# One pool per kind of tile, the rare path at the kernel's end, and the first attention in other PSUM banks

## The chip, the cores and the metric

The kernel runs on one core of a Trainium2 chip. Times are device microseconds (us) of one execution of the whole program. The engines are TensorE (PE in the profile, with PEld its weight loads), VectorE (DVE), ScalarE (ACT), GpSimd (POOL) and SyncE (SP), which issues nearly all transfers. Each engine works through its own list of instructions in order and waits on semaphores for the others. Engine names with a q behind them (PEq, SPq) stand for the engine's sequencer: branches, register loads and DMA issues.

## The reference

One layer of a hybrid decoder: 4096 tokens of width 1024, three mixers in parallel on one normalised input, then one output projection.

```python
def _hybrid_layer(x, c_act, ...):
    shift, scale, gate = jnp.split(c_act @ ada_w + ada_b, 3, axis=-1)
    h = _rmsnorm(x, g_pre) * (1.0 + scale[:, None]) + shift[:, None]
    aq, ak, av, ag, rkv, rg, gq, gkk, gv, gg = jnp.split(h @ w_in, ...)
    attn = _sliding_window_attention(aq, ak, av, sinks) * jax.nn.silu(ag)     # window 128, 8 heads of 64, 2 kv heads
    rwkv = _rwkv7_mixer(h, ...) * jax.nn.silu(rg)                             # a recurrence over the tokens, 4 heads
    gla = _gla_mixer(h, gq, gkk, gv, gk1, gk2, gk_b, gla_norm_w) * jax.nn.silu(gg)
    y = jnp.concatenate([attn, rwkv, gla], axis=-1) @ w_out
    return x + gate[:, None] * _rmsnorm(y, g_post)
```

RWKV-7 and GLA carry a state along the 4096 tokens; the attention looks at most 128 tokens back, with a sink per head in its softmax.

## The kernel before

The 4096 rows are worked through in 16 steps (NS) of 256 rows (NT). **Phase one** does for each step the normalisation (hT, the transposed input, is also stored in HBM), the projections of the two recurrent mixers, GLA, and RWKV-7 in chunks of 64 tokens. Of RWKV-7 the prediction names these pieces. PE forms products AT; these go through HBM (`adr`) into the layout AS; DVE solves a triangular system in a loop of small steps (`tsc`, `TT`); the result goes through HBM again (`tdr`, `td`); DVE transposes it (`D`), PE multiplies it out (`Xp`, `Xq`, `X`), and stage q2 runs four chained chunks (`rp`, `up`, `sp`) that carry the state. At its end DVE normalises `ysb`, PE transposes it (`yt`), ACT scales it, DVE adds the bonus `bon`, and the result of the step is stored (`mscr`). The last `yt`, of step 15, is thus the last that the recurrence asks of PE. Phase one also writes the weights of phase two to HBM in two f16 halves, high and low (`wscr`, `woscr`).

**Phase two** loads these weights (`stage_w`, L1594: q0 to q6, of which q5 and q6 lie in a pool of their own, `wg`) and does for each step: `qkv` (L1636: keys kp, queries qp in two halves with q0 and q1, values vp with q2; the values go through HBM, `vscr`, into four blocks v), `gates` (L1688: products gp with q3 to q6, tanh on ACT and one multiply on DVE into `ag`), `stage_s` (L1705: for each half a of the step the scores sc, a reduction on DVE that adds the bias `ab` and finds the maximum m, exponentials on ACT, division and transposes on DVE, and the product with the values, ovp), `stage_m` (L1790: the mixers' outputs times the gates, a scale found with a small product mp, and a split into f16 blocks `mtp`) and `outp` (L1877: seven products op per step in place of eight, combined on DVE in yv, normalised and stored).

The work is written as generators, one per stage, which `streams` and `emit` (L551) run interleaved by a model of the banks and the clock. Every instruction is noted by `Order`, whose `pin` (L205) fixes each engine's order by a list schedule with the kernel's own costs; it is called once for phase one and once for the loop of phase two. Step 0's attention, the projections of steps 0 and 1 and the gates of step 0 (`stage_first`) lie between the two; their places come from the scheduler of the framework, which puts them among the instructions of phase one as far as their tiles' ground, their banks and the barriers allow. Since the calls go through one helper, nearly all instructions carry its line, L334.

Tiles of SBUF come from pools. A pool of phase two that lies over ground of phase one can be filled when the tiles beneath are done with. Phase one has four pools by hand-made groups (`work1a` to `work1d`) and `c1p`; phase two has seven, each with several kinds of tiles. PSUM banks go by tags: `pj` (two), `at`, `sq`, `tr`, `m`, `y`, `mq`. Stage q2 uses `sq` and `y`.

A flag `fi` says if GLA's gates stay within a limit. If they don't (in none of the runs here), a **fallback** computes GLA again token by token, stores it to `mscr`, and loads again the three weight tiles that it used as work space. Its place is between the first attention and the loop of phase two: `values_load(fi)` at L2013, the branch at L2029, its loop at L2037. All engines pass the branch.

Of the kernel before, what the change touches and what calls it, by code (L numbers as in the profile page):

```python
# [11 lines left out]
F16 = mybir.dt.float16  # L12
# [284 lines left out]
class Model:  # L297


    def __init__(self, tc):  # L300
        self.tc, self.lift, self.stage, self.order = tc, 0, None, Order(tc)
        self.wrote, self.read, self.banks = {}, {}, {}
        self.now = self.pipe = 0.0
        self.shared = True
        self.gate = None
# [93 lines left out]
def hybrid_kernel(ctx, tc, x, vecs, rows, ada1, adaw, w1, wl, w2, wo, w2aug, a2, gk2, cst, ctr, ctg, abias, out):  # L399
# [84 lines left out]
    def pst(tag, name, bufs=1):  # L484
        t = ps.tile([P, 512], F32, tag=tag, name=name, bufs=bufs)
        model.take(tag, bufs, t.tensor.name)
        return t
# [67 lines left out]
    def emit():  # L555

        while live:
# [13 lines left out]
            model.lift, model.stage = LIFT.get(best[2], 0), best[2]  # L571
# [73 lines left out]
    with ExitStack() as p1:  # L645

        wk1 = [pool_of(p1, f"work1{n}", 1) for n in "abcd"]
        pp = pool_of(p1, "c1p", 1)
        order = (("hf", "gl", "b1", "zs", "gw", "cgc", "bl", "gk1s", "zl0", "zl1", "zl2", "ch", "cl", "cs"),
                 ("zb0", "zb1", "zb2", "ta", "ep", "em", "b2", "KB"),  # L650
                 ("qg", "kg", "egp", "egm", "vg", "c2", "kt", "cd", "em0"))

        def wt(shape, name, bufs=1, dt=F32, tag=None):
            tag = tag or name
            n = next((n for n, tags in enumerate(order) if tag in tags), 3)
            return wk1[n].tile(shape, dt, tag=tag, name=name, bufs=bufs)
# [68 lines left out]
        gvh = wk1[0].tile([P, KD, 272], F16, name="gvh")  # L725
        gvl = wk1[0].tile([P, KD, 272], F16, name="gvl")
# [850 lines left out]
    w2k, pp, wg, w2m, w2p, w2o, wb = [pool2(n) for n in ("work2k", "c2p", "wg", "work2m", "work2p", "work2o", "wb")]  # L1577
    pools = {"q": w2k, "kT": w2k, "vt": w2k, "v4": w2k, "mxa": w2m, "mxb": w2m, "pr": w2p, "yv": w2o, "sm1": w2o}
# [7 lines left out]
    ab = pp.tile([P, 8, 256], BF16, name="ab")  # L1586
# [7 lines left out]
    def stage_w(_):  # L1594
# [4 lines left out]
        for n in order:  # L1599
            slot = wslot if n < 5 else lambda name: wg.tile([P, KD, 256], F16, name=name)  # L1600
            got[n] = load_2(n, slot(f"q{n}h"), slot(f"q{n}l"))
            if n == 1:
                load_h(1)
# [32 lines left out]
    def qkv(i):  # L1636
# [10 lines left out]
        lohi = (slice(0, 64), slice(64, 128))  # L1647
        if i > 0:
            G.tensor_copy(kT[:, :, :, 0:P], F[i - 1]["kT"][:, :, :, NT : NT + P])
        yield ["pj"]  # L1650
        kp = pjt("kp")
# [10 lines left out]
        for n in range(2):  # L1662
            yield ["pj"]
            qp = pjt("qp")
# [9 lines left out]
        yield ["mq"]  # L1674
        vp = mq("vp")
# [5 lines left out]

        SP.dma_start(vscr[i].rearrange("(a p) c -> p a c", p=P), vt_)
# [3 lines left out]
        done.add(("qkv", i))  # L1686

    def gates(i):  # L1688
        yield [("og", i - 1)]
        f = F[i]  # L1690
        ag = t_A([P, 8, NT], "ag") if i == 0 else F[0]["ag"]
        f["ag"] = ag
        for n in range(4):
            yield ["pj"]
            gp_ = pjt("gp")
            for b in range(2):
                yield from proj(gp_[:, b * NT : (b + 1) * NT], Wq[3 + n], b * P, P, f["hT"])
# [5 lines left out]
        done.add(("gates", i))  # L1703

    def stage_s(i):  # L1705
# [4 lines left out]
        yield [q, kT, "at", "sq"]  # L1710
# [3 lines left out]
        for a in range(2):  # L1714
            first = i == 0 and a == 0
            k0 = P if first else 0
            pr = [wt([P, 4, 256], "pr", 3) for _ in range(2)]
            m = st.tile([P, 8], F32, tag="m", name="m")
            for jp in range(2):
                for kv in range(2):  # L1720
                    sc = pst(("at", "sq")[kv], "sc").rearrange("p (j n) -> p j n", j=2)
                    for jj in range(2):
                        for z in range(2):
                            PE.matmul(sc[:, jj, k0:], q[:, kv, 2 * jp + jj, a * P : (a + 1) * P],
                                      kT[:, kv, z, a * P + k0 : a * P + 256], start=(z == 0), stop=(z == 1))
                    for jj in range(2):
                        h = kv * 4 + 2 * jp + jj
                        V.tensor_tensor_reduce(pr[kv][:, 2 * jp + jj, k0:], sc[:, jj, k0:], ab[:, h, k0:], scale=1.0,
                                               scalar=sinks[:, h : h + 1], op0=ALU.add, op1=ALU.max,
                                               accum_out=m[:, h : h + 1])  # L1730
                if jp == 0:
                    yield ["at", "sq"]
            nm = st.tile([P, 8], F32, tag="nm", name="nm")
            V.tensor_mul(nm, m, fneg)
            es = st.tile([P, 8], F32, tag="es", name="es")
            V.tensor_sub(es, sinks, m)
            V.tensor_mul(es, es, lsc)
            sm = st.tile([P, 8], F32, tag="sm", name="sm")
            for h in range(8):
                S.activation(pr[h // 4][:, h % 4, k0:], pr[h // 4][:, h % 4, k0:], AF.Exp, bias=nm[:, h : h + 1],  # L1740
                             scale=lsc[:, h : h + 1], accum_out=sm[:, h : h + 1])
                if h % 2:
                    yield [sm]
            S.activation(es, es, AF.Exp)
            V.tensor_add(sm, sm, es)
            rd = st.tile([P, 8], F32, tag="rd", name="rd")
            V.reciprocal(rd, sm)
            for h in range(8):
                V.tensor_scalar(pr[h // 4][:, h % 4, k0:], pr[h // 4][:, h % 4, k0:], rd[:, h : h + 1], None, op0=ALU.mult)
                if h % 4 == 3:  # L1750
                    yield [pr[h // 4]]

            pT = []
            for kv in range(2):
                pT.append(wt([P, 4, 256], "pr", 3))
                if first:
                    for j in range(4):
                        V.transpose(pT[kv][:, j, k0:], pr[kv][:, j, k0:])
                else:
                    V.transpose(pT[kv].rearrange("p j n -> p (j n)"), pr[kv].rearrange("p j n -> p (j n)"))  # L1760
            tags = ("tr", "m", "y", "mq")
            yield [*pT, *v4, *tags]
            ov = [pst(tag, "ovp")[:, 0:P].rearrange("p (j n) -> p j n", j=4) for tag in tags]

            lo = 4 if first else 0
            joint()
            for d in range(5):
                for n in range(4):
                    if n + d < lo:
                        continue  # L1770
                    vt_, z = vblk[a + (n + d) // 4], (n + d) % 4
                    for kv in range(2):
                        PE.matmul(ov[n][kv * 64 : kv * 64 + 64], vt_[32 * n : 32 * n + 32, z, kv * 64 : kv * 64 + 64],
                                  pT[kv][32 * n : 32 * n + 32, :, 32 * (n + d) : 32 * (n + d) + 32],
                                  start=(n + d == max(lo, n)), stop=(d == 4))
            joint(False)
            for n in range(4):
                S.copy(mx[:, 0:4, a * P + 32 * n : a * P + 32 * n + 32], ov[n])
            yield ["at", "sq"]

    def block(i, n):
# [6 lines left out]
        V.scalar_tensor_tensor(t[:, 1], f["src"][n], f["msc"], t[:, 0], op0=ALU.mult, op1=ALU.subtract)  # L1788

    def stage_m(i):  # L1790
# [25 lines left out]
        mp = mq("mp")  # L1816
        PE.matmul(mp[:, 0:2], ones, mss, start=True, stop=True)
        mtot = st.tile([P, 1], F32, tag="mtot", name="mtot")
        V.tensor_reduce(mtot, mp[:, 0:2], axis=AX.X, op=ALU.add)
        msc = f["msc"] = st.tile([P, 1], F32, tag="msc", name="msc")  # L1820
        miv = st.tile([P, 1], F32, tag="miv", name="miv")
        pow2(msc, miv, mtot)
        oi = f["oi"] = st.tile([P, 1], F32, tag="oi", name="oi")
        V.tensor_mul(oi, miv, w_inv[7])
# [26 lines left out]
    def last_square(f, h, part, sums):  # L1851
# [3 lines left out]
        S.activation(f["junk"][:, 0:512], f["yv"][h][:, cols], AF.Square, scale=f["oi32"], accum_out=sums[:, part : part + 1])  # L1855
        V.tensor_tensor(z[:, cols], f["yv"][h][:, cols], gn[:, cols], op=ALU.mult)
# [20 lines left out]
    def outp(i):  # L1877
# [5 lines left out]
        yv = [wt([P, D], "yv", 2) if i < NS - 1 else  # L1883
# [35 lines left out]
        if end:  # L1919
            f["yv"], (f["junk"], *f["end"]) = yv, [wt([P, 4, 256], "pr", 3).rearrange("p j n -> p (j n)") for _ in range(3)]  # L1920
# [30 lines left out]
        else:  # L1951
            norm(i, 1, yv[1], x2[:, 0:D], f["blk"][5])
# [6 lines left out]
        else:  # L1959
            norm(i, 0, yv[0], x2[:, 0:D], f["blk"][6])  # L1960
        done.add(("o", i))

    def norm(i, a, yv, xt, junk):
        oi = F[i]["oi"]
# [39 lines left out]
    for n, stays in PRODUCTS:  # L2004
        if stays:
            Wr[n] = wb.tile([P, KD // 2, 4, 2, P], F16, name=f"o{n}")
# [165 lines left out]
```

## Time and profile before

| | before |
|---|---|
| median of 3 runs | 2091.4 us (2088.39 to 2092.16) |
| the profiled execution's own time | 2093.64 us |
| its span | 2091.8 us |
| mean granted clock of PE | 0.978 |
| PE busy | 1961.3 us, 94% of the span |
| DVE busy | 1612.5 us, 77% |
| ACT busy | 1154.3 us, 55% |

The profile is of one execution. A row of the timeline has start, duration, engine, line, operation, output and inputs, shape and, in brackets, how long the engine had been idle and who released it. A row of the waits has the waiting instruction, the releaser, the sum in us, the count and the longest. A matmul's own duration is longer than the distance to the next, since they are pipelined. Phase one lasts to about 1094 us, the loop of phase two from about 1133 us.

### The profile page before, as it was taken

To read this page: it belongs to the slowest core of one execution; us is meant where nothing else is said; L and a number is where in the kernel's file an instruction comes from. 1 tells how busy PE (TensorE), PEld (TensorE's weight loads), DVE (VectorE), ACT (ScalarE), POOL (GpSimd) and SP (SyncE) were. 2 spreads that over 40 slices of the span, in tenths; PEclk is the share of its full clock that TensorE was granted. 3 is DMA by queue.
4 is the path that set the end of the run, shared out by engine and by line. 5 is a ranking of instruction groups with operands and counts; after the bars stand their busy time and mean duration, and the time that the engine had idled before them with its cause. 6 is when DMAs were issued, how large, how long until landed. Compare 5 with 4: busy or idle time off the path is not lost. (4 is left out here: it accounts for less than half of the span.)

```text
span 2091.8 us, 61571 instructions
## 1 busy us (share of the span) xinstructions
PE 1961.3 (94%) x24931; PEld 1521.0 (73%) x24931; DVE 1612.5 (77%) x5211; ACT 1154.3 (55%) x2765; POOL 216.3 (10%) x405
## 2 busy tenths in 40 slices
PE   5899999999999999999876999999999999999997
PEld 2677778787787778777655767777877777877783
DVE  5677888878877688987745888777778777778777
ACT  4867676677776866765424444534444444344543
POOL 0511121421111111111100000000000000000000
PEclk9899999999999999999978999999999999999999
DMA  9332233323323312444116343433343433343314
GB/s 334 127 94 84 73 102 93 97 94 110 93 84 101 113 56 75 118 151 143 41 54 193 129 157 105 135 104 123 112 144 114 135 105 114 113 143 119 130 44 172
DMA packets 183894, 241.95 MB, mean 116 GB/s; under 512 B 52195, under 2 KB 141748, under 8 KB 179382
## 3 DMA queue, kind: packets, MB, share of 16 engines
q1 hardware_dynamic: 183462, 237.45, 35.2%
q8 instruction: 197, 3.23, 0.6%
q14 instruction: 91, 0.75, 0.1%
q10 hardware_dynamic: 144, 0.52, 0.1%
HBM read 177.08 MB, written 60.82 MB: 114 GB/s over the span
## 5 line engine op out<-in xcount | busy, mean ns | idle before, releaser
L334 PEld LDWEIGHTS <-mtp 128*128 128x128 f16 x1344 | 130.3, 98 | 141.3 <-issue 3.4
L334 PE MATMUL op<-o,mtp 128*128 128x512 f16 x768 | 172.1, 379 | 0.1
L334 ACT ACTIVATE pr<-pr,nm,lsc 128x256 f32<-128x256 f32 (+1 forms) x256 | 149.2, 585 | 36.0 <-DVE nm L334 35.9
L334 PE MATMUL op<-ov,mtp 128*128 128x512 f16 x576 | 143.4, 379 | 0.5 <-DVE q L334 0.5
L334 PEld LDWEIGHTS <-hT 128*128 128x128 f16 x1536 | 119.0, 100 | 25.9 <-issue 4.0
L334 DVE CUSTOM_DVE_ANT_0 pr<-sc,ab,sinks 128x256 f32<-128x256 f32 (+1 forms) x256 | 108.0, 475 | 14.1 <-PE sc L334 11.5
L334 DVE TENSOR_TENSOR yv<-op,yv 128x512 f32<-128x512 f32 x105 | 70.4, 681 | 48.6 <-PE op L334 34.3
L334 PE MATMUL pv<-gvh,hT 128*128 128x272 f16 x512 | 98.8, 283 | 6.6 <-DVE kg L334 3.1
L334 ACT ACTIVATE ag<-gp,gh 128x512 f32<-128x512 f32 x64 | 43.7, 683 | 102.8 <-PE gp L334 102.8
L334 POOL COPY kT<-kT 128x512 f16<-128x512 f16 x15 | 9.7, 646 | 872.7 <-DVE kT L334 820.5
L334 ACT ACTIVATE mtp<-yv,oi 128x1024 f16<-128x1024 f32 x30 | 34.3, 1143 | 112.6 <-DVE yv L334 112.6
L334 PE MATMUL lp<-hT,Lh 128*128 128x256 f16 x512 | 93.5, 276 | 0.1
L334 PE MATMUL gp<-hT,q3h 128*128 128x256 f16 x512 | 87.5, 275 | 4.4 <-PEq L2029 3.5
L334 PE MATMUL gp<-hT,q5h 128*128 128x256 f16 x512 | 91.1, 279 | 0.1
L334 PE MATMUL zz<-hT,rh 128*128 128x256 f16 x512 | 90.8, 277 | 0.0
L334 PE MATMUL zz<-hT,vh 128*128 128x256 f16 x512 | 88.8, 273 | 1.9 <-DVE zb L334 1.9
L334 PE MATMUL zz<-hT,kh 128*128 128x256 f16 x512 | 89.8, 273 | 0.0
L334 PE MATMUL gqk<-hT,gqkh 128*128 128x256 f16 x512 | 89.6, 276 | 0.0
L334 DVE SCALAR_TENSOR_TENSOR ag<-ag,gp 128x512 f32<-128x512 f32 x64 | 43.7, 683 | 58.5 <-ACT ag L334 58.2
L334 PE MATMUL qp<-hT,q0h 128*128 128x256 f16 x512 | 85.3, 273 | 2.3 <-DVE yv L334 1.5
L334 PE MATMUL qp<-hT,q1h 128*128 128x256 f16 x512 | 86.2, 273 | 0.0
L334 PE MATMUL gp<-hT,q6h 128*128 128x256 f16 x512 | 85.3, 273 | 0.0
(460 smaller groups left out, 6048.5 us busy)
## 6 DMA issues: line engine op xcount, KB each, us to landing
ov<-woscr SPq DMA_DIRECT2D x96, 512.0 KB, 4.0
xt<-in_x SPq DMA_DIRECT2D x16, 1024.0 KB, 5.1
hscr<-hT SPq DMA_DIRECT2D x16, 1024.0 KB, 5.0
hT<-hscr SPq DMA_DIRECT2D x16, 1024.0 KB, 4.8
x<-in_x SPq DMA_DIRECT2D x30, 512.0 KB, 4.5
out<-yv SPq DMA_DIRECT2D x30, 512.0 KB, 2.9
cs<-in_w SPq DMA_DIRECT2D x112, 128.0 KB, 2.4
v<-vscr SPq DMA_DIRECT2D x128, 64.0 KB, 2.6
```

The source lines that it names most:

```text
L334: r = f(*args, **kw)
```

## The change

**Pools.** Both phases now have one pool for each kind of tile. The pools of phase one stand in a list, and those of phase two in another, so that phase two's tiles lie over particular tiles of phase one: `q` over gvh and gvl, the weights q5 (`w5`) over b1, gl, bl, cs, ch, gw, the weights q6 (`w6`) over gw, zs and gaw, and so on. `yv` moves to ground that the input's tiles had (`t_A`), `mtp` to a pool.

**Banks.** Step 0's attention has its scores in `at` and `tr` in place of `at` and `sq`, and its ovp in `at`, `tr`, `m`, `mq` in place of `tr`, `m`, `y`, `mq`. The values vp of steps 0 and 1 use `pj`.

**Gates.** There are two buffers for `ag`; `gates(i)` asks that the gating of step i−2 be done, where it asked for i−1.

**Fallback.** It stands behind the loop of phase two. As the output is by then computed, it does all of phase two again as well, after GLA. For that `attend`, `heads_of`, `gates_of`, `spread_values` and `mix_scale` are made functions of their own, and `norm` gets its destination as an argument; the work they do in the main path is that of before.

```diff
     with ExitStack() as p1:
-        wk1 = [pool_of(p1, f"work1{n}", 1) for n in "abcd"]
-        pp = pool_of(p1, "c1p", 1)
-        order = (("hf", "gl", "b1", "zs", "gw", "cgc", "bl", "gk1s", "zl0", "zl1", "zl2", "ch", "cl", "cs"),
...
+        soon = ("w2s", "w0s", "a2s", "CT", "CTG", "scolb", "uw", "w0p0", "w0p1", "one16", "mu_s", "mu_c", "a0h")
+        late = ("td", "tf0", "tf1", "Sst0", "Sst1", "lnx")
+        tags = ("gvh", "gvl", "hf", "b1", "gl", "bl", "cs", "ch", "gw", "zs", "gaw", "gacc", "zl0", "zl1", "zl2", "early",
+                "zb1", "ta", "em", "ep", "zb0", "b2", "zb2", "kg", "kt", "egm", "egp", "qg", "vg", "c2", "middle",
+                "AS", "osb", "c3", "KB", "ATm", "c1", "RA", "UV", "BK", "cd", "em0", "bon", "ysb", "rs", "Ss", "lasts")
+        wk1 = {n: pool_of(p1, f"work1{n}", 1) for n in tags}
...
-    w2k, pp, wg, w2m, w2p, w2o, wb = [pool2(n) for n in ("work2k", "c2p", "wg", "work2m", "work2p", "work2o", "wb")]
-    pools = {"q": w2k, "kT": w2k, "vt": w2k, "v4": w2k, "mxa": w2m, "mxb": w2m, "pr": w2p, "yv": w2o, "sm1": w2o}
+    pools = {n: pool2("work2" + n) for n in (
+        "q", "kT", "vt", "w5", "w6", "ab", "v4", "pr", "mxa", "ag", "mtp", "mxb", "sm1", "o1", "o6", "o4", "o5", "ov")}
...
-            slot = wslot if n < 5 else lambda name: wg.tile([P, KD, 256], F16, name=name)
+            slot = wslot if n < 5 else lambda name: pools[f"w{name[1]}"].tile([P, KD, 256], F16, name=name)
...
     def gates(i):
-        yield [("og", i - 1)]
+        yield [("og", i - 2)]
         f = F[i]
-        ag = t_A([P, 8, NT], "ag") if i == 0 else F[0]["ag"]
-        f["ag"] = ag
+        f["ag"] = ag = t_A([P, 8, NT], "ag") if i == 0 else pools["ag"].tile([P, 8, NT], F32, name="ag2") if i == 1 else F[i - 2]["ag"]
+        yield from gates_of(f["hT"], ag, pjt)
...
     def stage_s(i):
         yield [("qkv", i), ("s", i - 1), ("o", i - 2)]
-        yield [q, kT, "at", "sq"]
+        sct, ovt = (("at", "tr"), ("at", "tr", "m", "mq")) if i < 1 else (("at", "sq"), ("tr", "m", "y", "mq"))
+        yield [q, kT, *sct]
...
         for a in range(2):
+            yield from attend(q, kT, vblk, mx, a, i == 0 and a == 0, sct=sct, ovt=ovt)
...
+    model.order.forget()
+    x2 = t_x("x2")
+    xo, gn = x2[:, 0, :], x2[:, 1, :]
+    mtp = pools["mtp"].tile([P, 4, 2, 4, P], F16, name="mtp")
...
+    streams((0, "v", stage_v, None), *((1, "s", stage_s, i) for i in range(1, NS)), *((2, "m", stage_m, i) for i in range(NS)),
+            *((3, "p2", stage_p2, i) for i in range(NS)))
+    emit()
+    model.order.pin()
 
     flag = nc.values_load(fi[0:1, 0:1], min_val=0, max_val=1)
...
     with tc.If(flag == 0):
...
-        for t, n in tiles_o[:3]:
-            load_o(t, n)
...
+        with tc.For_i(0, NS, 1) as iv:
+            SP.dma_start(fh.rearrange("p a k t -> p (a k t)"), hscr[bass.ds(iv, 1)].rearrange("o p n -> p (o n)"))
+            run(heads_of(fh, fq, fkT, fvt, pjt, mq))
+            spread_values(fvt, fv[1:], 0)
+            run(gates_of(fh, F[0]["ag"], pjt))
...
```

What this does to the order of the instructions shows at three places. The first is **SP**, around the triangular solve of step 14 and ahead of that of step 15. Before, with the loads of q5 and q6 only behind the `td` of step 15:

```order
L334 DMA adr<-AT 16x8x16 x5
L334 DMA AS<-adr 64x256 x2
L334 DMA q3h<-wscr 128x2048
L334 DMA q3l<-wscr 128x2048
L334 DMA q4h<-wscr 128x2048
...
L334 DMA td<-tdr 16x8x16 x8
L334 DMA adr<-AT 16x8x16 x8
L334 DMA AS<-adr 64x256 x2
...
L334 DMA td<-tdr 16x8x16 x2
L334 DMA q5h<-wscr 128x2048
```

After the change:

```order
L334 DMA adr<-AT 16x8x16 x5
L334 DMA q5h<-wscr 128x2048
L334 DMA q5l<-wscr 128x2048
L334 DMA AS<-adr 64x256 x2
L334 DMA q3h<-wscr 128x2048
...
L334 DMA vscr<-vt 128x2x128
L334 DMA v_18959<-vscr 32x4x128
L334 DMA adr<-AT 16x8x16 x8
L334 DMA v_18959<-vscr 32x4x128 x3
L334 DMA AS<-adr 64x256 x2
L334 DMA v_18960<-vscr 32x4x128 x4
```

The load of q5 now stands between step 14's adr and its AS, and the values of step 0 are stored and loaded around step 15's. The second place is **PE**, at the end of step 0's attention, where the branch stood:

```order
L334 MATMUL sc<-kT,q 128x256
L334 MATMUL ovp<-pr,v_18758 64x128 x14
L334 MATMUL ovp<-pr,v_18759 64x128 x2
...
L334 MATMUL ovp<-pr,v_18759 64x128 x14
L2013 TENSOR_LOAD fi
L2029 COMPARE_AND_BRANCH
```

In the changed kernel the second half's ovp follows the values of step 1, and other work follows it:

```order
L334 MATMUL qp<-hT,q1l 128x256
L334 LDWEIGHTS hT
L334 MATMUL vp<-q2h,hT 128x128
...
L334 MATMUL vp<-q2h,hT 128x128
L334 MATMUL ovp<-pr,v_18959 64x128 x14
L334 MATMUL ovp<-pr,v_18960 64x128 x2
```

The third is **DVE**, in the last normalisation of ysb, that of step 15. Before:

```order
L334 SCALAR_TENSOR_TENSOR ag<-ag,gp 128x512
L334 TENSOR_TENSOR ysb<-ysb,yr 128x512
L334 TENSOR_TENSOR ysb<-ysb,bon 128x512
L334 SCALAR_TENSOR_TENSOR kT<-kp,kq_s,kT 64x256 x4
L334 ISA pr,m<-sc,ab,sinks 128x128
```

The same place of DVE in the changed kernel:

```order
L334 SCALAR_TENSOR_TENSOR kT<-kp,kq_s,kT 64x256
L334 SCALAR_TENSOR_TENSOR yr<-nwt,yr 128x8
L334 SCALAR_TENSOR_TENSOR kT<-kp,kq_s,kT 64x256
L334 TENSOR_TENSOR nwt<-yr 128x8
L334 SCALAR_TENSOR_TENSOR nwt<-nwt,ve 128x8
L334 SCALAR_TENSOR_TENSOR yr<-nwt,yr 128x8
L334 TENSOR_TENSOR ysb<-ysb,yr 128x512
L334 SCALAR_TENSOR_TENSOR q<-qp,q 64x512
L334 TENSOR_TENSOR ysb<-ysb,bon 128x512
L334 SCALAR_TENSOR_TENSOR q<-qp,q 64x512
L334 ISA pr,m<-sc,ab,sinks 128x256
```

Splits of keys, which came behind the recurrence, now stand between the small instructions of its normalisation (`nwt`, `yr`), and the reductions (ISA) after it are those of the second half; the first half's stand earlier, in the triangular loop of step 15. From the first gate product with q3 behind the second mp on, the order of PE is the same in both until the last step; there it differs a little.

274 lines of the change are left out of this document (161 added, 113 removed).

## The prediction

> **What bounds the kernel now.** I read the page's busy shares first, then its 40 slices, then the windows table to find where TensorE (PE) loses time.
>
> ```profile
> span 2091.8 us, 61571 instructions
> PE 1961.3 (94%) x24931; PEld 1521.0 (73%) x24931; DVE 1612.5 (77%) x5211; ACT 1154.3 (55%) x2765; POOL 216.3 (10%) x405
> PE   5899999999999999999876999999999999999997
> PEclk9899999999999999999978999999999999999999
> ...
> 1000.00:1100.00 100.00, 80.85 (x1276) 61.30 (x1275) 53.78 (x195) 30.31 (x67) 7.58 (x14) 0.85 0.14 40
> 1100.00:1200.00 100.00, 81.81 (x881) 63.52 (x879) 72.53 (x225) 44.16 (x124) 1.71 (x2) 0.90 0.49 160
> 1300.00:1500.00 200.00, 197.36 (x2098) 151.73 (x2097) 154.58 (x426) 87.59 (x222) 1.84 (x3) 1.00 0.36 119
> ```
>
> PE bounds the steady part: 197.36 of 200 us from 1300. (The numbers of such a row are the window's length, each engine's busy time with its count, PE's granted clock and the DMA share and rate.) The one hole is the passage between the phases, slices 20 to 22: 19 us of idle PE in each of the two windows there, and a granted clock of 0.85 and 0.90. The waits of PE from 1000 to 1180 name what it stands behind, the timeline where:
>
> ```profile
> PE ovp L334 <- DVE pr L334: 11.1, 4, 9.6
> ...
> 1093.65 0.66 PE L334 MATMUL yt<-ident,ysb 128*128 128x128 f32 x4 [0.74 <-DVE ysb L334]
> 1126.29 0.70 PE L334 MATMUL ovp<-pr,v 32*64 32x128 f32 x6 [9.56 <-DVE pr L334]
> 1133.44 0.59 PE L334 MATMUL gp<-hT,q3h 128*128 128x256 f16 x2 [3.54 <-PEq L2029]
> ...
> 1222.47 2.02 PE gp L334 x17
> ```
>
> The yt transposes at 1093.65 are the last of step 15's recurrence; after them nothing of phase one holds PE. The last row, of the chain of waits, is the first gate product from which both kernels issue PE's work in the same order. So I cut the run at two points: up to yt, and from yt to 1222.47. The windows of the second stretch, PE alone:
>
> ```profile
> core 0: us, PE busy (x), PEclk, DMA share, GB/s
> 1093.65:1222.47 128.82, 108.50 (x1083) 0.92 0.49 157
> 1093.65:1116.73 23.08, 19.80 (x225) 1.00 0.69 201
> 1116.73:1139.36 22.63, 9.04 (x132) 0.55 0.38 129
> 1139.36:1222.47 83.11, 79.66 (x727) 1.00 0.46 153
> ```
>
> In the 22.63 us in the middle PE works 9.04, at clock 0.55: there it waits for the second half of step 0's attention (9.56) and for the branch at L2029 (3.54), and gives back the clock. With nothing else queued on PE ahead of the branch, no other work can fill that.
>
> **The change, part by part.** *Moved ahead of yt.* Counting PE's matmuls in both orders, the changed kernel issues before the last yt what stood behind it: the values of step 0 (48), half a set of queries (48) and the first scores. The pitches come from these rows: 48 products of 128 columns from 1096.67 to 1099.35, 2.68 us; 120 of 256 columns in 13.12 us, 0.109 each; 22 of 512 columns in 4.75, 0.216 each.
>
> ```profile
> 1096.67 0.22 PE L334 MATMUL vp<-q2h,hT 128*128 128x128 f16 x1 [0.51 <-ACT ysb L334]
> ...
> 1099.35 0.38 PE L334 MATMUL qp<-hT,q0h 128*128 128x256 f16 x2
> ...
> 1134.24 5.12 PE vp L334 x48
> 1147.94 13.12 PE gp L334 x120
> 1208.30 4.75 PE op L334 x22
> ```
>
> By them the counted work from yt to the common point is 98.1 us before and 87.7 after: 10.4 us have moved. Ahead of yt they cost nothing, since PE idles there for most of the 10 us of the first two windows below:
>
> ```profile
> 1050.00:1055.00 5.00, 2.18 (x8) 0.50 0.16 22
> 1055.00:1060.00 5.00, 1.14 (x5) 0.50 0.47 127
> 1060.00:1065.00 5.00, 4.80 (x167) 0.57 0.95 346
> 1070.00:1075.00 5.00, 5.00 (x55) 0.50 0.01 3
> 1075.00:1080.00 5.00, 5.00 (x71) 0.71 0.00 0
> ```
>
> *The hole after yt.* In the new order some 9.2 us of PE work (48 products of q1, 4 scores, 48 values) lie between yt and the second half's ovp. That ovp needs the chain of VectorE (DVE) and ScalarE (ACT) behind yt:
>
> ```profile
> 1094.35 2.28 ACT L334 ACTIVATE ysb<-yt,lnx 64x256 f32<-64x256 f32 x4 [2.78 <-PE yt L334]
> ...
> 1115.99 0.08 DVE L334 DVE_READ_ACCUMULATOR2_ANT m<- 128x1 f32 x1
> ...
> 1124.90 2.52 DVE L334 STREAM_TRANSPOSE pr<-pr 128x1024 f32<-128x1024 f32 x2
> ...
> L334 DVE CUSTOM_DVE_ANT_0 pr<-sc,ab,sinks 128x256 f32<-128x256 f32 x40 | 17.3, 481 | 8.6 <-PE sc L334 6.4 <-issue 1.1 <-PE ovp L334 0.9
> L334 DVE SCALAR_TENSOR_TENSOR q<-qp,q 64x512 f16<-64x512 f32 x12 | 8.3, 688 | 2.4 <-ACT q L334 2.1
> L334 DVE SCALAR_TENSOR_TENSOR kT<-kp,kq_s,kT 64x256 f16<-64x256 f32 x10 | 4.8, 484 | 1.7 <-ACT kT L334 1.6
> ```
>
> ACT copies to 3.0 us after yt; bonus and two q splits (0.69 each) and the last four reductions (0.48) bring it to 6 or 7; from the last reduction to ovp the old trace takes 10.3 us (1115.99 to 1126.29). So ovp starts some 17 us after yt, PE is out of work at 9.2, and a hole of about 8 us stays, against 9.56 and 3.54 and some shorter ones now.
>
> The second stretch then sums to: 87.7 of work; 5.4 that PE's busy time holds beyond the counted work (108.50 less 98.1 is 10.4, of which I put 5 down to the cold middle window); 8 for the hole; 2.4 for a cold clock behind it (the 48 values at 1134.24 took 5.12 instead of 2.68); 3.5 of stalls on DVE, as the last of the windows has them (83.11 less 79.66). That is 107.0. DVE used some of the idle time to get ahead and now lacks it: nothing to 5 us, of which I take 1.5. Sum 108.5 instead of 128.8: **a gain of 20.3**, bounds 16 (all 5 us of the stalls, a hole of 9) and 26 (no cold clock, a hole of 5). The loads of the output weights, which SP now issues behind the td of step 15 instead of behind the values, are hidden: the first output product comes 20 us or more after the values.
>
> [...]
>
> *The recurrence up to yt.* Step 15's Xp-to-up stretch runs at clocks 0.57, 0.50 and 0.71 in the rows above. At full clock their 4.80, 5.00 and 5.00 us would be 6.0 shorter; fresh PE work right ahead should give part of it, and I take 4.8 (bounds 0 and 6.0). The eight ab multiplies leave the way of the D transpose, which they hold for 2.19 us:
>
> ```profile
> 1057.39 2.19 DVE L334 TENSOR_SCALAR ab<-a,fiv 128x256 bf16<-128x256 f32 x8 [2.82 <-PE kp L334]
> ...
> 972.65 0.38 SPq L334 DMA_DIRECT2D woscr<-ch  x1
> ...
> 976.65 1.34 SPq L334 DMA_DIRECT2D AS<-adr  x2
> ...
> 1057.38 0.34 SPq L334 DMA_DIRECT2D q5h<-wscr  x1
> ...
> 1103.26 5.51 SPq L334 DMA_DIRECT2D v<-vscr  x8
> ```
>
> I take 1.8. Against it: q5h and q5l now stand on SP ahead of AS of step 14 (two issues at 0.34 are the floor, and a wait for their ground comes on top; 0.7 to 4, I take 2). vscr and the first values stand ahead of adr of step 15, three more ahead of its AS (5.51/8 each: 0.7 to 3.1; 0.6, as SP waits for AT there anyway). Four kT splits inside ysb's normalisation are 1.9 us, of which 1.2 is not in the gaps; eight half-width reductions (0.48 each at most) stand in step 15's triangular loop in place of two gate multiplies, which I put at 1. Sum: −4.8 −1.8 +2 +0.6 +1.2 +1 = **−1.8**, bounds −6 and +4.
>
> *The branch.* It now stands behind all work:
>
> ```profile
> 2085.05 3.71 SPq L334 DMA_DIRECT2D out<-pr  x4
> 2086.49 1.42 DVE L334 SCALAR_TENSOR_TENSOR pr<-pr,ln,xo 128x512 f32<-128x512 f32 x2
> ```
>
> DVE's last work ends at 2087.9, the span at 2091.8, so about 3 us of landing can cover most of a branch that PE pays with 3.54 and SP reaches last, behind the out transfers. I take +1.2, bounds 0 and 4. [...]
>
> *At nothing.* Two gate buffers, the other banks and the new pools leave the steady loop's rows as they were on every engine, and PE leaves 2.6 us of 200 there. The last step's order differs a little: ±1. If the pools held a load back by a shared neighbour, PE's 197.36 would show it.
>
> Sum: −20.3 −1.8 +1.2 = −20.9. The profiled execution took 2093.64, its span lies 1.84 below, the median of the runs shown 2.24 below. 2093.64 − 20.9 = 2072.7, so **2070** as a median (rounded from 2070.5).
>
> **The rivals.** *More than that.* The clock stays up through the recurrence (6.0) and the hole shrinks to 5, because the second half's scores run under phase one: −30, 2061. For it: DVE is busy only 53.78 of 100 us from 1000. Against it: the chain behind yt is serial, 17 us of rows.
>
> *The loads and values on SP get into the recurrence.* SP's instructions wait in order, and adr, AS, tdr and td are on it for every step. If the ground of q5 and q6, or the values of step 0, come 8 to 10 us late, half the gain goes: 2081.
>
> The same mechanism is the **slower** case: a weight load that waits ahead of AS of step 14 for ground that step 14 itself frees late. It stands in front of AS, the triangular loop and step 15. It decides from 21 us of hold; 26 would give 2096. Against it: the store of ch, one of the last readers of the ground that q5 takes, is issued at 972.65, 4 us ahead of AS.
>
> *No change.* The gain of the passage is given back as stalls on DVE up to 1222.47, DVE being busy 72.53 of 100 and ACT 44.16: 2090. It would need all of the 20 us, with some 27 of DVE idle there. Also here: the branch ends up still inside the passage, which PE's order speaks against.
>
> **How the numbers follow.** Forecast (2063 to 2078) 0.58; more 0.16; SP loads at half the gain 0.13; no change 0.06; slower 0.07. One measurement tells about 0.2%, ±4 us, from no change. The first three are faster: 0.87; same 0.06; slower 0.07. The range takes in the first two rivals and leaves out no change and the slower case: 2056 to 2086.
>
> **What would show it.** After the change there is no L2029 row among PE's waits, and one gap of 6 to 10 us ahead of ovp; the third slice of the passage loses its dip in PEclk to one window near 0.5. From yt to the gate product of 17 pieces 106 to 111 us; yt itself 0 to 5 us earlier. In windows from 1300 on PE stays at 98.7%. I am wrong if yt comes later than 1095 (SP or DVE order), if PE's waits behind DVE from the passage on exceed 12 us beside the hole, or if ovp waits over 12 us.

## The result and the profile after

The changed kernel takes 2070.11 us (median; 2069.16 to 2070.41) beside 2091.78 for the kernel before (2088.39 to 2093.88) on the same chip: a ratio of 0.9897, 95% interval 0.988 to 0.9914. The profiled execution took 2070.41 us, 23.2 less than that of before, with a span of 2068.6. Its page, the lines that answer to those of before:

```profile
span 2068.6 us, 61564 instructions
PE 1954.1 (94%) x24931; PEld 1516.6 (73%) x24931; DVE 1610.2 (78%) x5211; ACT 1154.7 (56%) x2765; POOL 216.6 (10%) x405
PE   5899999999999999999888999999999999999997
PEclk8999999999999999999999999999999999999999
```

The dip of slices 20 to 22 has gone from 8, 7, 6 to three times 8, and the clock shows none. Behind the last yt, the windows of PE (length, busy time with its count, granted clock, DMA share and rate), its waits (sum, times, longest), and rows of its timeline, with one of the chain of waits as the last:

```profile
core 0: us, PE busy (x), PEclk, DMA share, GB/s
1092.02:1197.55 105.53, 95.41 (x939) 0.95 0.44 148
1104.00:1118.00 14.00, 8.44 (x117) 0.63 0.39 141
1118.00:1197.55 79.55, 76.63 (x704) 1.00 0.41 135
```

```profile
PE ovp L334 <- DVE pr L334: 6.3, 2, 5.1
PE gp L334 <- DVE yv L334: 1.4, 1, 1.4
```

```profile
1092.02 0.66 PE L334 MATMUL yt<-ident,ysb 128*128 128x128 f32 x4 [1.34 <-DVE ysb L334]
1107.94 0.70 PE L334 MATMUL ovp<-pr,v 32*64 32x128 f32 x8 [5.06 <-DVE pr L334]
1109.93 2.41 PE L334 MATMUL ovp<-pr,v 32*64 32x128 f32 x72 [1.29 <-DVE pr L334]
...
1197.55 2.02 PE gp L334 x17
```

From yt to the gate product at which both orders join: 105.53 us instead of 128.82, a gain of 23.3. Up to yt it is 1.6 less (1092.02 against 1093.65), from that product to the end of the span 1.7 more (871.05 against 869.33). −23.3 −1.6 +1.7 is the whole difference of the spans, 23.2. No row of PE's waits names a branch any more, and the hole ahead of the second half's ovp is 5.06 us.

Ahead of yt, in the windows that ran at clocks 0.57, 0.50 and 0.71 before, the clock is full:

```profile
1060.00:1065.00 5.00, 3.90 (x92) 1.00 0.20 57
1070.00:1075.00 5.00, 4.98 (x102) 1.00 0.02 3
1075.00:1080.00 5.00, 5.00 (x85) 1.00 0.02 3
```

The steady loop did not move: from 1300 to 1900 the waits of PE hold the same one row as before.

```profile
PE sc L334 <- DVE m L334: 8.8, 10, 0.9
```

### The profile page after: what moved, and what is told of

It reads as the page before. It is cut to its first block, busy times and chain, and to the rows that moved or that the text cites. A ratio compares the mean times of both kernels' runs of the same rounds, so it can differ in the third digit from the quotient of the medians.

```text
span 2068.6 us, 61564 instructions
## 1 busy us (share of the span) xinstructions
PE 1954.1 (94%) x24931; PEld 1516.6 (73%) x24931; DVE 1610.2 (78%) x5211; ACT 1154.7 (56%) x2765; POOL 216.6 (10%) x405
## 4 chain that ended last, share of the span: by engine, by line
PE 57%; DVE 24%; DMA 8%; ACT 6%; issue 3%; SPq 2%; DVEq 0%; POOL 0%; ACTq 0%; POOLq 0%
PE gp L334 16%; PE op L334 12%; PE zz L334 5%; PE qp L334 3%; PE lp L334 3%; PE sc L334 2%; SPq L334 2%; DVE mtp L334 2%; DVE q L334 2%; PE ovp L334 2%; PE kp L334 2%; DVE pr L334 2%; PE pv L334 2%; DMA cs<-in_wo 1%; DMA cs<-in_w 1%
## 5 line engine op out<-in xcount | busy, mean ns | idle before, releaser
L334 ACT ACTIVATE ag<-gp,gh 128x512 f32<-128x512 f32 x64 | 43.7, 683 | 109.4 <-PE gp L334 109.4
```

Of the source, the lines that this page charges most:

```text
L334: r = f(*args, **kw)
```

## The experiments

All are told by four stretches of their profiled executions, in us: from the start of AS of step 14 on SP to tdr of step 15; from there to the last yt; from yt to the end of the span; and the tail, from the end of DVE's last instruction to the end of the span. The last columns are the median and the ratio to the kernel before, timed beside each.

| | AS to tdr | tdr to yt | yt to end | tail | median | ratio (95%) |
|---|---|---|---|---|---|---|
| before | 72.3 | 44.7 | 998.2 | 3.89 | 2091.78 | |
| before without branch | 68.7 | 43.0 | 991.8 | 3.65 | 2083.91 | 0.9959 (0.9944 to 0.9973) |
| changed | 76.1 | 39.0 | 976.6 | 5.63 | 2070.11 | 0.9897 (0.988 to 0.9914) |
| changed, second time | 76.9 | 39.0 | 976.4 | 5.90 | 2073.20 | 0.9902 (0.9884 to 0.9921) |
| changed, third time | 76.5 | 39.0 | 976.8 | 5.71 | 2069.54 | 0.989 (0.987 to 0.9909) |
| branch in the middle | 71.1 | 41.4 | 979.9 | 3.94 | 2070.65 | 0.9886 (0.9855 to 0.9916) |
| no branch | 72.6 | 39.0 | 974.3 | 3.66 | 2067.61 | 0.9871 (0.984 to 0.9901) |
| old banks | 73.8 | 38.7 | 987.0 | 5.68 | 2078.45 | 0.9935 (0.9911 to 0.9959) |
| one gate buffer | 76.1 | 39.0 | 975.9 | 5.90 | 2073.22 | 0.9891 (0.9867 to 0.9916) |
| q5 behind AS | 78.0 | 39.0 | 976.0 | 5.87 | 2069.57 | 0.9889 (0.9868 to 0.991) |
| orderings on SP | 71.5 | 39.0 | 978.4 | 5.91 | 2068.76 | 0.9892 (0.9865 to 0.9919) |
| a quarter of the gates early | 78.1 | 39.0 | 972.4 | 5.66 | 2067.91 | 0.9885 (0.9862 to 0.9907) |
| all the gates early | 76.3 | 39.0 | 992.0 | 5.67 | 2085.87 | 0.9966 (0.9948 to 0.9985) |
| orderings and a quarter of the gates | 74.1 | 39.0 | 972.1 | 5.55 | 2065.99 | 0.9869 (0.9846 to 0.9893) |

The times of one kernel spread by up to 15 us over its runs in the later series. Some of that arises far ahead of the change: the same program reaches AS of step 14 between 976.9 and 978.8 us in three executions, and its variants between 971.1 and 981.2. What comes behind yt repeats within 0.5 us (976.6, 976.4, 976.8). So the medians decide what moves 5 us or more, and the stretches decide the rest. Kernels with the same order up to yt differ by 3.6 us between AS and tdr (72.3 and 68.7), so that column decides little.

**The branch put back in the middle.**

```diff
+    yvs = t_A([P, 2, D], "yv")
+    F[0]["yv"] = [yvs[:, a, :] for a in range(2)]
+    flag = nc.values_load(fi[0:1, 0:1], min_val=0, max_val=1)
+    with tc.If(flag == 0):
...
     model.order.forget()
     x2 = t_x("x2")
...
     model.order.pin()
-    flag = nc.values_load(fi[0:1, 0:1], min_val=0, max_val=1)
-    with tc.If(flag == 0):
...
```

> The changed kernel with the fallback put back between the first attention and the loop of phase two (as the old short one, GLA alone and three reloaded tiles); pools, banks and gate buffers stay changed. TensorE's order up to the second half's ovp is that of the changed kernel, so theory 1 (most of the gain is work moved under the recurrence and a shorter chain behind yt; the branch's place alone is a small term) expects yt within 1 us of 1092, a stall of some 3.5 us at the branch, some 2 us for work that can't pass it, and 1.7 us back at the end where the branch is gone: 2074, between 2072 and 2077. Rival (the place of the branch is what brought the gain, since nothing could fill the hole across it): 2084 or more.

The time, 2070.65, is under the range of theory 1 and 13 us under the rival's, so the branch's place is not what brought most of the gain. Behind yt its price is about as expected all the same, and a shorter time ahead of yt made up for it. The waits of PE behind yt in this kernel:

```profile
PE ovp L334 <- DVE pr L334: 6.4, 2, 5.1
PE sc L334 <- PEq L2060: 3.9, 1, 3.9
PE sc L334 <- DVE m L334: 1.3, 1, 1.3
```

The branch costs PE 3.95 us, and from yt to the end of the span it takes 979.9 instead of 976.6: +3.3, where 3.5 + 2 − 1.7 was expected. But AS to yt is 112.4 us here instead of 115 to 117, a difference of the size of the scatter named above. In the timelines of SP 2.2 us of it lie between tdr and td of step 14:

```profile
1000.86 1.11 SPq L334 DMA_DIRECT2D tdr<-TT  x2
1003.95 3.65 SPq L334 DMA_DIRECT2D td<-tdr  x8
```

```profile
1001.26 1.11 SPq L334 DMA_DIRECT2D tdr<-TT  x2
1003.03 0.43 SPq L334 DMA_DIRECT2D x<-in_rows  x1
1006.58 3.82 SPq L334 DMA_DIRECT2D td<-tdr  x8
...
1001.52 0.35 ACTq L1620 DMA_DIRECT2D x<-gscr  x1
```

```profile
SPq L334 <- DMA tdr<-TT: 3.0, 1, 3.0
```

The first fence is the kernel with the branch in the middle, the other two the changed one, its timelines and a wait of SP: there td is issued 4.2 us behind the end of tdr's issue instead of 2.0, since tdr itself takes longer to land: 4.7 us at the longest, and SP waits 3.0 for it, where the kernel with the branch in the middle has no row of such a wait. The rows that the changed kernel has in that place, and this one only behind its branch, are a load of x on SP and one on ACT's own queue, the row of the gate broadcast to all partitions (x<-gscr). The ordering experiment below tells these two apart.

**The kernel before without its branch.**

```diff
-    flag = nc.values_load(fi[0:1, 0:1], min_val=0, max_val=1)
-    with tc.If(flag == 0):
...
     model.order.forget()
     x2 = t_x("x2")
```

> The kernel before without the fallback and its branch (what the kernel would do where the flag is 0 is left out; the flag is still computed). TensorE's order then puts 21 gate products (2.3 us) ahead of the second half's ovp and the rest as before. Theory 1: 3.5 us of the branch, 2.3 of the hole and 1 or 2 of later overlap go: 2084 to 2086. Rival (branch brought the gain): 2074 or less. Both would leave yt at 1093 to 1095.

The time is 2083.91, just under theory 1's range and 10 us over the rival's. yt came at 1090.0, 3 us earlier than expected, with an order up to there that is that of before. From yt to the end it takes 991.8 us instead of 998.2. Its waits of PE behind yt show what is left without the branch:

```profile
PE ovp L334 <- DVE pr L334: 8.8, 4, 7.3
PE sc L334 <- DVE m L334: 2.7, 4, 0.9
```

The hole has shrunk by the 2.3 us of gate products that now stand in it, from 9.56 to 7.3. Behind yt the branch in the middle costs 6.3 us against none in the old order, and 5.6 in the new one (979.9 above, and 974.3 in the kernel with no branch below); at the end instead of the middle, as in the changed kernel, it is worth 3.3. Each of these is the smaller part of the 21.6 us that the change gains there.

**The old banks.**

```diff
-        sct, ovt = (("at", "tr"), ("at", "tr", "m", "mq")) if i < 1 else (("at", "sq"), ("tr", "m", "y", "mq"))
+        sct, ovt = ("at", "sq"), ("tr", "m", "y", "mq")
-        yield from heads_of(hT, q, kT, vt_, pjt, mq if i > 1 else pjt)
+        yield from heads_of(hT, q, kT, vt_, pjt, mq)
```

> The changed kernel with step 0's attention in the banks of before (scores in at and sq, ovp in tr, m, y, mq, values in mq). TensorE's order puts all scores of step 0 behind the recurrence's last chunk and both halves' ovp behind yt. Theory 1: the chain of two halves of attention on DVE and ACT then stands behind yt, ovp of the second half 25 to 30 us after yt instead of 18, and the time is 8 to 12 us longer: 2080, between 2076 and 2084. Rival (the pools and the branch brought it, the banks little): 2070, within 2 us.

The time is 2078.45, within theory 1's range and over 6 us above the rival's. The timeline of PE behind its yt at 1089.23:

```profile
1099.65 1.01 PE L334 MATMUL sc<-kT,q 128*128 128x256 f16 x4 [4.23 <-DVE m L334]
1103.82 2.98 PE L334 MATMUL ovp<-pr,v 32*64 32x128 f32 x40 [1.15 <-DMA v<-vscr]
1118.80 0.69 PE L334 MATMUL ovp<-pr,v 32*64 32x128 f32 x6 [4.77 <-DVE pr L334]
```

The first half's ovp, of which in the changed kernel 24 of 40 matmuls run under the recurrence, comes 14.6 us behind yt, and the second half's 29.6, instead of 15.9. The stretch behind yt grows by 10.4 us, and takes more than the hole itself shows, 4.77, because scores wait for reductions before it (4.23). The sq bank is also that of the recurrence's chunks: in the kernel before, which has these banks too, 4 scores of step 0 stand at 1038.27 and all others from 1087.39 on, behind the last sp (1086.7), while in the changed kernel 28 of 32 stand ahead of yt, the first at 1021.56. The edit puts back the banks of the scores, of ovp and of the values, so the 10.4 us belong to the three together; they are the largest single part of the gain. The median grew by less, 8.3 us, as AS to yt takes 112.4 us here.

**No branch at all.**

```diff
     model.order.pin()
-    flag = nc.values_load(fi[0:1, 0:1], min_val=0, max_val=1)
-    with tc.If(flag == 0):
...
```

> The changed kernel without the fallback and its branch (what it would do where the flag is 0 is left out). Theory 1: from DVE's last work to the end of the span 3.9 us as in the kernel before, 1.7 less than in the changed one: 2068.4. [...] Rival b (the last transfers cover the branch): 2070.

The tail, of the changed kernel and of this one, is read from the end of DVE's last instruction (the start of its row plus 1.42) to the end of the span, 2068.6 and 2067.1:

```profile
2061.55 1.42 DVE L334 SCALAR_TENSOR_TENSOR pr<-pr,ln,xo 128x512 f32<-128x512 f32 x2
```

```profile
2062.02 1.42 DVE L334 SCALAR_TENSOR_TENSOR pr<-pr,ln,xo 128x512 f32<-128x512 f32 x2
```

They are 5.63 and 3.66: the branch at the end costs 2.0 us, near theory 1's 1.7, and half of what PE waited for it in the middle (3.54 before, 3.95 above). That the landing of the last transfers covers the other half fits this and is not shown by a row. The median, 2067.61, lies 0.8 under theory 1's and decides nothing.

**One gate buffer.**

```diff
-        yield [("og", i - 2)]
+        yield [("og", i - 1)]
-        f["ag"] = ag = t_A([P, 8, NT], "ag") if i == 0 else pools["ag"].tile([P, 8, NT], F32, name="ag2") if i == 1 else F[i - 2]["ag"]
+        f["ag"] = ag = t_A([P, 8, NT], "ag") if i == 0 else F[0]["ag"]
```

> The changed kernel with one gate buffer, the gates of a step waiting for the gating of the step before. Theory 1: the steady loop was bound by TensorE at 98.7% before with one buffer, so nothing: 2070, within 1.5 us. Rival (the second buffer lets the gates of step 1 start in the passage and takes 2 to 4 us of its stalls): 2072 to 2074.

Behind yt it takes 975.9 us, slightly less than the changed kernel's 976.4 to 976.8. The median, 2073.22, lies where the rival had it, but the changed kernel in the same series has 2073.20. The second buffer gains nothing by itself, as theory 1 had it.

**q5 behind AS.**

```diff
+                if i == NS - 2:
+                    model.hold = r.ins.name
...
-        SP.dma_start(h.rearrange("p k c -> p (k c)"), wscr[n, :, 0])
+        r = SP.dma_start(h.rearrange("p k c -> p (k c)"), wscr[n, :, 0])
+        if n == 5:
+            tc.add_manual_dep(
+                r.ins, model.hold, mybir.DependencyInfo(mybir.DependencyClass.NoSync, mybir.DependencyReason.DATA))
```

The first lines stand in the loop that loads AS.

> The changed kernel with one added ordering: the load of q5 (and with it what follows) is issued behind AS of step 14, as in the kernel before. The flag's transpose on TensorE came 2.4 us later in the changed kernel (992.2 against 989.8) at the same rows ahead. Theory 1 (q5 ahead of AS holds step 14's solve up by about 2 us, and step 15 and yt with it): that transpose back to 990, yt 2 us earlier, 2068. Rival (the recurrence has slack there or the loads cost it elsewhere): 2070, within 1 us.

The order bound the first of q5's two loads only; the other, q5l, stayed ahead of AS, so this is half of the edit that was meant. The flag's transpose came at 985.4, but this execution had reached adr of step 14 six us earlier already (964.83 against 971.15), before q5 could matter, so that mark decides nothing. From the end of adr's issues to the start of AS it is 1.15 us here, 1.18 in the changed kernel (adr's last row 973.36 + 2.38, AS 976.92) and 1.17 before (up to 3.3 in other executions, but 3.0 also in the kernel before without its branch), so q5 is not seen to hold up the issue of AS. But the data of AS come later behind it. These are the first steps of the solve, in the kernel before, in this one and in the changed one:

```profile
980.42 0.17 DVE L334 TENSOR_TENSOR tsc<-TT,AS 128x16 f32<-128x16 f32 x1
975.97 0.18 DVE L334 TENSOR_TENSOR tsc<-TT,AS 128x16 f32<-128x16 f32 x1 [0.90 <-POOL AS L334]
982.78 0.18 DVE L334 TENSOR_TENSOR tsc<-TT,AS 128x16 f32<-128x16 f32 x1 [1.83 <-POOL AS L334]
```

From the end of adr's issues to that step it takes 4.9 us before (6.4 without its branch), 6.0 here with one load of q5 ahead of AS, and 7.0, 8.4 and 7.4 in the three executions of the changed kernel with both, where POOL waits for AS to land until then (1.94 us in the first of them, to 982.62). From that step to tdr every kernel takes 18.2 to 18.8 us. So the first pair of profiles has the solve start 2.1 us later, as theory 1 had it, and over all these executions the difference is 0.6 to 3.5 us. The cause, q5's two loads of 512 KB ahead of AS, is read from the order and not tested cleanly. AS to tdr is no shorter here (78.0), and the time is the rival's: what half the edit could give is lost in the rest of the stretch.

**The orderings on SP.**

```diff
+                if i == NS - 1:
+                    model.hold_as = r.ins.name
...
+                    if i == NS - 2:
+                        model.hold_td = r.ins.name
...
+            if a == 0:
+                tc.add_manual_dep(
+                    r.ins, model.hold_td, mybir.DependencyInfo(mybir.DependencyClass.NoSync, mybir.DependencyReason.DATA))
...
+        if v4 is F[0].get("v"):
+            tc.add_manual_dep(
+                r.ins, model.hold_as, mybir.DependencyInfo(mybir.DependencyClass.NoSync, mybir.DependencyReason.DATA))
```

The four pieces stand behind the loads of AS, behind those of td, behind the load of x from in_rows, and behind the store vscr.

> The changed kernel with two orderings added on SP: the first row of the loop of phase two (x from in_rows) is issued behind td of step 14, and the values of step 0 (vscr and their loads) behind AS of step 15; TensorE's order is that of the changed kernel. In the changed kernel td of step 14 is issued 4.2 us after tdr (1.7 before the change) and AS of step 15 6.7 us after the start of adr (4.9 before). Theory 1 (both stand ahead of the recurrence on SP and hold it up): td 1.5 to 2 us after tdr, AS within 5.4 us of adr, from AS of step 14 to yt 3 to 4 us less (112 instead of 115 to 117), the stretch behind yt as it is: 2066 to 2068. Rival (the recurrence has that much slack there, its other chain over the chunks of step 14 sets yt): the two gaps shrink, from AS of step 14 to yt stays at 115, 2070.

The timeline of SP in this kernel, and ACT's own queue:

```profile
1000.48 1.10 SPq L334 DMA_DIRECT2D tdr<-TT  x2
1006.09 3.64 SPq L334 DMA_DIRECT2D td<-tdr  x8
1025.55 3.63 SPq L334 DMA_DIRECT2D adr<-AT  x8
1030.33 1.11 SPq L334 DMA_DIRECT2D AS<-adr  x2
```

```profile
1000.75 0.35 ACTq L1624 DMA_DIRECT2D x<-gscr  x1
```

Half of the expectation holds. With the values behind it, AS of step 15 starts 4.8 us after adr, where the changed kernel has 6.7: 1.9 us that the three loads between took. (The kernel without a branch and the one with the branch in the middle have three loads there too, and 5.3 us.) But td is still 4.5 us behind the end of tdr's issue, with no load of x ahead of it. What remains beside tdr is the broadcast of the gate row on ACT's queue, which the old kernel issued behind its branch (1133.54) and the one with the branch in the middle at 1115.66. So the 3 us that tdr lands late point to that transfer, which the prediction did not list. In all eleven executions with the new pools and no branch ahead of the loop, td starts 4.1 to 4.7 us behind the end of tdr's issue, and the broadcast starts 0.26 to 0.27 behind tdr in the changed kernel, in this one and in the one with both edits below; in the other three executions td starts 1.4 to 2.0 behind it. It was not moved by itself, so this is an inference.

From AS to yt it takes 110.5 us, 4.6 to 6.7 less than in the seven executions with the changed kernel's SP order and branch at the end. Not all of that is the orderings': 2.4 of the 4.6 us to the first profile lie between AS and tdr of step 14, ahead of what they moved, and the same order has 24.9 us there instead of 21.9 in the kernel with both edits below. From td of step 14 to tdr of step 15 it takes 43.9 us here and 43.7 there, against 45.5 to 48.9 in the seven; but the kernel without a branch, with that SP order too, has 43.1. So a gain of some 2 us there is likely and not shown. The time, 2068.76 beside 2069.54, tells nothing; 1.7 us went behind yt on a wait for a weight load that the changed kernel does not have:

```profile
PE op L334 <- DMA ov<-woscr: 1.7, 1, 1.7
```

**Gates of step 1 earlier.** First all four quarters:

```diff
         yield from qkv(1)
+        yield from gates(1)
...
-        if i in (1, NS - 1):
+        if i == NS - 1:
             yield from gates(i)
```

> The changed kernel with the gates of step 1 computed among the first work, ahead of the loop of phase two, which the second gate buffer allows. TensorE's order puts 24 gate products (2.6 us) and 7 more around the first ovp of the second half, where it now stands idle for 5.1 and 1.3 us and then runs at clock 0.50 for 5 us. Theory 1 (the hole is idle TensorE time, and filling it keeps the clock up): hole 2 to 3 us, clock in the window 1110 to 1115 above 0.8, 4 us gained: 2066, between 2064 and 2068. Rival (behind yt the chain of DVE and ACT sets the end whatever TensorE does; the gates' multiplies lengthen it): 2070 to 2073.

The hole went, and the time did not follow: 2085.87, ratio 0.9966 (0.9948 to 0.9985), 992.0 us behind yt. What this kernel puts out departs from the layer, for a cause that stayed open, so its time counts only as that of this order of work. Its waits of PE from yt to 1230 us:

```profile
PE sc L334 <- DVE m L334: 5.4, 6, 2.5
PE op L334 <- DMA ov<-woscr: 3.0, 1, 3.0
PE mp L334 <- ACT mtp L334: 2.9, 2, 2.5
PE gp L334 <- ACT vt L334: 2.1, 1, 2.1
PE op L334 <- ACT mtp L334: 2.1, 1, 2.1
```

All 192 gate products now precede the scores of step 1, so DVE and ACT idle first and are waited for later: from 1115 to 1135 us DVE works 4.5 of 20 us and ACT 3.5, where the changed kernel has 16.5 and 11.8 from 1112 to 1132. Then a quarter, 48 products with q3:

```diff
         yield from qkv(1)
+        yield from gates(1, range(1))
...
-            yield from gates(i)
+            yield from gates(i, range(1, 4) if i == 1 else range(4))
```

> The changed kernel with the first quarter of the gates of step 1 (48 products with q3, 5.25 us) computed ahead of the loop of phase two; the other three quarters stay in it. TensorE's order then has 31 of them around the first ovp of the second half and 17 behind it, then the scores of step 1. Theory 1 (TensorE's 5.1 and 1.3 us of idle time there, and 2 us of cold clock behind it, are real losses): the hole under 2 us, PEclk not under 0.8 after it, from yt to the end of the span 972 us instead of 976.5, 2066. Rival (what held all four quarters moved back, 992 us behind yt, is that the scores of step 1 come late for DVE and ACT; it holds for one quarter too): 976 or more, 2070 or more.

Theory 1 holds to half a us behind yt: 972.4, 4.2 less. The median, 2067.91, is 2 us over its 2066 and 1.6 under the changed kernel's. The waits of PE behind yt and its windows there:

```profile
PE gp L334 <- ACT vt L334: 2.1, 1, 2.1
PE gp L334 <- DVE ag L334: 1.7, 1, 1.7
...
PE ovp L334 <- DVE pr L334: 0.9, 2, 0.7
```

```profile
1105.00:1110.00 5.00, 2.92 (x40) 1.00 0.93 331
1110.00:1115.00 5.00, 4.12 (x101) 1.00 0.44 165
1115.00:1120.00 5.00, 5.00 (x48) 1.00 0.28 81
```

Two gaps of 2.1 and 1.7 us leave the clock at 1.00, where the changed kernel with its gap of 5.06 runs at 0.52 and 0.50 from 1105 to 1115:

```profile
1105.00:1110.00 5.00, 0.78 (x15) 0.52 0.49 197
1110.00:1115.00 5.00, 4.67 (x84) 0.50 0.38 108
```

**Both edits**, the quarter and the orderings on SP:

> Both edits: the two orderings on SP, and the first quarter of the gates of step 1 ahead of the loop. Theory 1: their gains add, being in different stretches: 2062 to 2064. Rivals: whatever of the two gains nothing alone, gains nothing here.

Behind yt it takes 972.1 us, as with the quarter alone, and AS to yt 113.1. The median, 2065.99, is 2 us over the 2062 to 2064 of theory 1. It is 3.5 us under the changed kernel's beside it and the lowest of all here, though the intervals of the two ratios overlap (0.9846 to 0.9893 and 0.987 to 0.9909).

The **changed kernel again**, for the scatter:

> The changed kernel again, beside the three others on one chip: 2070, within 1 us, with yt at 1092 and the second half's ovp 16 to 18 us behind it.

> The changed kernel beside them: 2070 to 2073; from yt to the end of the span 976.5 us within 0.5, and from AS of step 14 to yt 111 to 117 us.

The stretch behind yt came within 0.5 us of 976.5 both times. The medians, 2073.20 and 2069.54, lay 2.2 us over and 0.5 under what was expected, and the first yt 1.6 us later, at 1093.64: the scatter again.

## Why the prediction was right, point by point

The forecast was 2070, from a gain of 20.9 in the profiled execution, and 2070.11 was measured, from 23.2. That the two agree to 0.1 us is luck: the gain was 2.3 us larger, and the runs' median lay 0.3 us below the profiled execution and not 2.24. By its own steps:

- **Work moved ahead of yt, the hole, the clock and the stalls (20.3): right, 23.3.** PE's busy time in the stretch was to be 87.7 + 5.4 + 2.4 = 95.5, and is 95.41. Its idle time was to be 8 + 3.5 + 1.5 = 13.0, and is 10.1: the hole is 5.06 + 1.29 = 6.4 instead of 8, as ovp comes 15.9 us behind yt and not 17 and PE has work for 10.9 us and not 9.2 (16 products ovp of the first half, at 1095.05, were not in the count); and DVE, robbed of its idle time, is not waited for longer. The 1.5 us for that were not needed. That the clock would be cold behind the new hole too (2.4) was the author's estimate from the old one of 9.56 us; behind the 5.06 it is 0.50 from 1110 to 1115. So two of its signs were missed on the good side: the gap ahead of ovp is under 6 us, and the stretch, 105.53, under 106.
- **The recurrence up to yt (−1.8): the sum fits one profile (−1.6) and is not shown by it.** The same programs scatter by more than that. Its two halves can be told apart better. The clock and the ab multiplies were to give 4.8 + 1.8 less 1.2 for the kT splits, 5.4 between tdr and yt: that stretch takes 38.7 to 39.0 us in every execution with the new pools but one, instead of 44.7 and 43.0. In the changed kernel the clock is full there (1.00 in each window of 5 us from 1050 to 1095). The one exception, 41.4 with the branch in the middle, stays open, and what the ab multiplies give was not told apart. The other half, 3.6 of new delays ahead of tdr, came out as 3.8, in part by luck. q5 (2) shows as 2.1 at the start of step 14's solve, though through the landing of AS and not through a wait on SP. The reductions in step 15's solve (1) show as 0.9: from its first step to tdr 16.63 us instead of 15.78. The values around adr and AS (0.6) cost 1.8 between adr and AS. A tdr that lands late stood nowhere in the sum, 2.6 us, and the time from td to the next adr, 3.0 us shorter (20.0 instead of 23.1), did not either, nor did 0.5 less between AS of step 15 and its first use. The kernel before without its branch has 20.4 there, so the 3.0 may be scatter, and how much of the late tdr reaches yt stays open.
- **The branch at the end (+1.2, 0 to 4): 1.7 to 2.0.** With the branch gone the tail is what it was before.
- **At nothing: right.** The loop's waits are the same to the tenth, and the end of the program less its tail is 865.4 us behind the joining point in both kernels. One gate buffer does as well as two.
- **What made it:** moving the branch to the end is worth 3.3 us in the new order, and the banks 10.4. Between the kernel before and the changed one, both without a branch, lie 17.5 us behind yt (991.8 and 974.3); the banks leave some 7 of them to the ground that is free earlier and to the scheduler's other moves, and those were not undone by themselves.
- **The rivals.** The larger gain did not come, since the hole stayed (5.06), though half of it could be had: the quarter of the gates shows 4.2 us. SP's loads did get into the recurrence's way, by about 2 us each at the two places that the prediction named and not by 8 to 10, and no weight load is seen to hold up the issue of AS. The gain was not given back as stalls on DVE.

## What to carry to other kernels

Where a serial phase hands over to a parallel one, price the handover as work that can move ahead of the last serial result and the chain that still hangs behind it. Here the banks that the serial phase holds counted for more (10.4 us) than the branch between the phases (3.3 to 6.3). Filling a hole on the bound engine pays only as long as what the other engines need next is not pushed back: 48 products gained 4.2 us, and 192 lost 15. To tell changes of a few us in a long program, compare stretches between fixed events of the traces, as the total scatters by what happens long before. And to see what a transfer put ahead of another costs, look at when the second one's data are used, not only at when it is issued: q5 left the issue of AS in place and its first use came 2.1 us later.

## What the runs showed of the hardware that was not expected

Two small transfers landed late beside large ones. tdr of step 14, two stores of 32 KB on SP's queue, took up to 4.7 us to land where a broadcast of 512 KB stood beside it on ACT's queue, and 1.9 at most in the kernel before. AS of step 14, two loads of 64 KB, landed in 2.4 us at most before; with q5's two loads of 512 KB ahead of it in the changed kernel, POOL waited for it until 982.62, 4.0 behind the start of its second load's issue (978.6). Both are read from where the transfers stand in these kernels: the broadcast was not moved by itself, and of q5 only one load. And a branch that nothing follows cost 2.0 us at the program's end where the same kind of branch in the middle stopped PE for 3.5 to 4.0.
